# A row-wise nan-max on one core: the first load issued as three strided parts instead of one

## The chip, the cores and the metric

The kernel runs on one core of a Trainium2 chip. The metric is the device time of one execution in microseconds. The kernel before takes 1251.33 us (median of three runs, 1251.32 to 1251.34).

Four engines of the core matter here: ACT (ScalarE), POOL (GpSimd) and DVE (VectorE) compute, and SP (SyncE) issues all transfers. The transfers are carried out by 16 DMA engines.

## The reference

The input x is 32 x 2048 x 2048 in float32, drawn from a normal distribution, with one value in ten replaced by NaN. The output is the maximum over the last axis without the NaNs:

```python
def reference(x: np.ndarray, axis: int) -> np.ndarray:
    return np.nanmax(x, axis=axis).astype(np.float32)
```

These are 65536 rows of 2048 values (8 KB each), 537 MB in all, and 0.26 MB of results.

## The kernel before

**Tiles.** The rows are laid out over 128 partitions in five groups (`GROUPS`), so that a partition holds a run of neighbouring rows. Tiles go over a group from left to right. The unit is a quarter row (`Q` = 512 values). `TILES` lists for each tile its loads, its key chunks, and its reductions, all in quarter rows. Tile 0 is small: one row per partition, `[4]`, which is 1 MB and one load. Most of the others have 28 quarter rows, seven rows per partition, 7 MB in one load. Towards the end the loads are cut ever smaller, down to a quarter row in the last tile.

**Work on a tile.** Three steps remove the NaNs in place. ACT makes a 16-bit key from the upper half of each value (`act` with Prelu, into `kts`). POOL, or ACT for some chunks, turns the keys back into the upper halves (`write`), in which a NaN has become a very low number. DVE reduces each row to its maximum (`maxima`, into `accs`). After a group's last tile, `find_part` marks rows that held nothing but NaN, and six stores write the results.

**Buffers.** Three buffers `xts` hold tiles in turn, and three buffers `kts` hold keys. A tile's load may start when the last reduction of the tile that had the buffer is through (`free`).

**Order.** Everything but the first load stands in one critical section in which the order on each engine and all semaphores are made by hand: `Order.add` issues an instruction with the waits that it needs. An instruction that waits for several semaphores gets a separate wait instruction for each but the last. Loads use 14 semaphores in turn, the lanes (`LANES`, `lanes`, `turn`): a load waits for the load that had its lane before it.

**The first load.** `HEADS` is 1: tile 0's load is issued by SP ahead of the section (line 269), with a dependence offset that keeps the framework from ordering it against the buffer's later uses. Then comes the barrier at which the section begins (line 276); the other engines and SP's next loads (line 466) start behind it. Within the section the loop over tiles takes the already issued instruction from `heads` and adds it to the order as a load on lane 0, so that tile 0's key pass (line 282) waits for that lane.

Of the kernel before, what the change touches and what calls it, by code (L numbers as in the profile page):

```python
# [9 lines left out]
D = 2048  # L10

Q = D // 4
# [55 lines left out]
WIDE = 7  # L68
# [5 lines left out]
LEAD = 128  # L74

HEADS = 1

LANES = 14

# [13 lines left out]
def joints(keys, backs, reds):  # L93


    parts = []
    pieces = []
    at = end = step = 0
    for n, wait in backs:
        end += n  # L100
        while at < end:
            at += keys[step]
            step += 1
        if wait is None or wait >= 0:
            parts.append((end - n, end, wait is not None, step + (wait or 0), len(pieces)))
        pieces.append(n)
    needs = []
    done = 0
    for n in map(abs, reds):
        over = [i for i, p in enumerate(parts) if p[0] < done + n and p[1] > done]  # L110
        done += n
        pools = [i for i in over if not parts[i][2]]
        acts = sorted((i for i in over if parts[i][2]), key=lambda i: parts[i][3])
        if pools and acts and parts[pools[-1]][3] > parts[acts[-1]][3]:
            acts = []
        needs.append(pools[-1:] + acts[-1:])
    pairs = {}
    for need in needs:
        if len(need) == 2 and all(sum(i in n for n in needs) == 1 for i in need):
            both = tuple(parts[i][4] for i in need)  # L120
            for i in both:
                pairs[i] = both
    return pairs
# [62 lines left out]
def kernel(  # L186
# [15 lines left out]
    nc = tc.nc  # L202
    P = nc.NUM_PARTITIONS
# [14 lines left out]
    for tiles in GROUPS:  # L218
        at = 0
# [8 lines left out]
    firsts = [  # L228
        nc.alloc_sbuf_tensor(f"xt{i}", [P, WIDE * D], i32).ap() for i in range(HEADS)
    ]  # L230
# [6 lines left out]
    xts = firsts + [  # L237
        sing.tile([P, WIDE * D], i32, name=f"xt{i}") for i in range(HEADS, BUFS)
    ]
# [10 lines left out]
    groups = []  # L250
# [12 lines left out]
    order = Order(nc)  # L263
    heads = []
    for number in range(HEADS):
        (c,) = TILES[number][0]
        gi, base = place[number]
        to = xts[number][:, 0 : c * Q]
        head = nc.sync.dma_start(  # L269
            out=dataclasses.replace(to, dep_tracking_offset=to.offset + P * WIDE * D),  # L270
            in_=groups[gi][0][:, base : base + c * Q],
        )
        tc.no_tile_sem_insts.add(head.ins.name)
        heads.append(head)

    with tc.tile_critical() as section:  # L276

# [52 lines left out]
        lanes = [[] for _ in range(LANES)]  # L330
        turn = 0
# [43 lines left out]
        def freed(*ks):  # L375

            uses = [(back, then, e) for k in ks for back, ((_, then), e) in kfree[k].items()]
            counts = [e[1] for _, _, e in uses if e[0] == "pool"]
            deps = []
            for back, then, e in uses:  # L380
                if back == "act" and order.count["act"] >= then:
                    e = ("act", then)
                if back != "pool" or e[0] == "pool" or all(v < then for v in counts):
                    deps.append(e)
            return deps
# [39 lines left out]
        def find_part(i):  # L425
            gi, lo, hi = spans[i]
            first = groups[gi][2]
            acc = accs[:, first + lo : first + hi]
            deps = [done_at[PARTS[i][2]]]
            if PARTS[i][3] == "dve":  # L430
                none = nones[:, 0 : hi - lo]
                ready[i] = find("dve", nc.vector, deps, acc, none, ALU.bitwise_or)
            else:
                none = late[:, 0 : hi - lo]
                ready[i] = find("pool", nc.gpsimd, deps, acc, none, ALU.add)

        for number, (loads, chunks, reds) in enumerate(TILES):
            keys = [k for ks, _ in chunks for k in ks]
            fresh = {}
            step = 0  # L440
            for ks, bs in chunks:
                assert sum(ks) * Q <= KEYS
                assert sum(ks) == sum(b[0] if isinstance(b, tuple) else b for b in bs)
                fresh[step] = sum(ks) * Q
                step += len(ks)
            backs = [b for _, bs in chunks for b in bs]
            backs = [b if isinstance(b, tuple) else (b, None) for b in backs]
            assert sum(loads) == sum(keys) == sum(b for b, _ in backs) == sum(map(abs, reds))
            pairs[number] = joints(keys, backs, reds)
            for i, part in enumerate(PARTS):  # L450
                if part[3] == number:
                    find_part(i)
            gi, base = place[number]
            xg = groups[gi][0]
            xt, before = xts[number % BUFS], free[number % BUFS]
            assert number < BUFS or state["tile"] > number - BUFS
            landed = []
            at = 0
            for c in loads:
                c *= Q  # L460
                e = order.add(
                    "sp",
                    nc.sync,
                    lambda: heads[number]
                    if number < HEADS
                    else nc.sync.dma_start(  # L466
                        out=xt[:, at : at + c], in_=xg[:, base + at : base + at + c]
                    ),
                    before + lanes[turn],
                    lane=f"load{turn}",  # L470
                    step=16,
                )
                lanes[turn] = [e]
                turn = (turn + 1) % LANES
                landed.append((at, at + c, e))
                at += c
            end = at
            at = lo = part = 0
            for step, c in enumerate(keys):
                c *= Q  # L480
                here = [l for a, b, l in landed if a < at + c and b > at]
                kold = []
                if used + fresh.get(step, 0) > KEYS:
                    key = (key + 1) % NKEYS
                    used = 0
                    assert all(h[3] != key for h in held)
                    assert all(q[2] != key for v in half.values() for q in v)
                    kold = freed(key, (key + 1) % NKEYS) if number in EARLY and at + c == end else freed(key)
                    kfree[key] = {}
                e_key = act(  # L490
                    kold + here,
                    out=kts[key][:, used : used + c],
                    in_=xt[:, at : at + c].bitcast(i16)[:, 1::2],
                    func=ACT.Prelu,
                    bias=EDGE,
                    scale=-1.0,
                    alpha=float(TOP - LOW) / (EDGE - NAN),
                )
                used += c
                at += c  # L500
                for h in held:
                    h[-1] -= 1
                for h in [h for h in held if h[-1] <= 0]:
                    held.remove(h)
                    write(*h[:-1], "act")
                while backs and lo + backs[0][0] * Q <= at:
                    n, wait = backs.pop(0)
                    n *= Q
                    kp = kts[key][:, used - (at - lo) : used - (at - lo) + n]
                    if wait is not None and wait > 0:  # L510
                        held.append([number, lo, lo + n, key, kp, e_key, part, wait])
                    else:
                        who = "pool" if wait is None else "act" if wait == 0 else "dve"
                        write(number, lo, lo + n, key, kp, e_key, part, who)
                    lo += n
                    part += 1
                if number == len(TILES) - 1 and at == end:
                    for h in held:
                        write(*h[:-1], "act")
                    held.clear()  # L520
                maxima(number)
            assert lo == end
# [5 lines left out]
        for (gi, lo, hi), e in zip(spans, ready):  # L528
            _, og, first, _ = groups[gi]
# [4 lines left out]
                    out=og[:, lo:hi], in_=accs[:, first + lo : first + hi].bitcast(i32),  # L534
# [3 lines left out]
                lane="store",  # L538
                step=16,
# [47 lines left out]
```

## Time and profile before

| | |
|---|---|
| median of three runs | 1251.33 us |
| the profiled execution's own time | 1251.31 us |
| its span, first to last instruction | 1249.7 us |
| DMA engines, share of the span | 99.5% |
| mean rate over the span | 430 GB/s |
| POOL busy | 93% |
| DVE busy | 89% |
| ACT busy | 78% |

The span runs from the first to the last instruction that the profiler saw; what lies between it and the execution's time (1.6 us) is around the kernel. Lines such as L269 are lines of the kernel. "SPq" is SP's queue of DMA issues: its durations are those of issuing, not of moving data. A row of the timeline gives start, duration, engine, line, operation, destination and source with their shapes, the number of merged instructions, and in brackets the idle time before it and what ended it. A row of the waits gives who waited for whom, the sum, the number of times and the longest wait. A row of the stages gives the stretch, its length, the busy time and count of DVE, ACT and POOL, the granted clock, the DMA engines' busy share and the rate. A packet counts with all its bytes and its whole time in the stage in which it starts, so in short stages a share can be above 1.

### The profile page before, as it was taken

What the parts mean: (1) busy time and instruction counts of PE and PEld (TensorE: products, weight loads), DVE (VectorE), ACT (ScalarE), POOL (GpSimd) and SP (SyncE); (2) the same over time, 40 slices, a digit from 0 to 9 for tenths busy, and PEclk for the clock granted to TensorE, in tenths of its full rate; (3) what the DMA queues carried; (4) which work ended last, traced back from release to release, by engine and by line L of the source; (5) the groups of instructions that cost most, each with busy time, mean ns of one, the idle gap of its engine ahead of it and who ended that gap; (6) DMA issues with size and microseconds to landing.
All of it is one profiled execution on the core that took longest, in us unless ns stands there. A gap on an engine that the chain in (4) does not pass through costs nothing.

```text
span 1249.7 us, 920 instructions
## 1 busy us (share of the span) xinstructions
DVE 1109.7 (89%) x184; ACT 980.1 (78%) x286; POOL 1158.9 (93%) x256
## 2 busy tenths in 40 slices
DVE  0888889888889888888988888988898999999999
ACT  3777777777777777777777777799877799999998
POOL 2999999999999999999999999967999987999998
DMA  9999999999999999999999999999999999999997
GB/s 415 441 428 424 441 441 437 415 441 441 439 426 428 441 439 433 422 439 441 439 426 428 441 439 435 426 433 441 439 428 426 441 437 431 425 436 428 429 428 313
DMA packets 16854, 537.19 MB, mean 430 GB/s; under 512 B 2640, under 2 KB 2640, under 8 KB 5200
## 3 DMA queue, kind: packets, MB, share of 16 engines
q1 hardware_dynamic: 16848, 537.14, 99.5%
q14 instruction: 6, 0.05, 0.0%
HBM read 536.87 MB, written 0.26 MB: 430 GB/s over the span
## 4 chain that ended last, share of the span: by engine, by line
POOL 34%; DVE 30%; DMA 26%; ACT 9%; issue 1%; SPq 0%
POOL xt L292 34%; DVE acc L299 30%; DMA xt<-in_x_dram 26%; ACT kt L282 7%; ACT xt L282 2%; POOL late L305 0%; POOL acc L319 0%; SPq L269 0%; SPq L466 0%; DVE none L305 0%; DVE acc L319 0%; SPq L582 0%; SPq L276 0%
## 5 line engine op out<-in xcount | busy, mean ns | idle before, releaser
L292 POOL TENSOR_SCALAR xt<-kt 128x3584 int16<-128x3584 uint16 (+10 forms) x241 | 1153.9, 4788 | 84.5 <-ACT kt L282 69.3
L299 DVE TENSOR_REDUCE acc<-xt 128x4 f32<-128x8192 f32 (+4 forms) x182 | 1109.4, 6148 | 137.5 <-POOL xt L292 130.6
L282 ACT ACTIVATE kt<-xt 128x3584 uint16<-128x3584 int16 (+10 forms) x252 | 913.9, 3663 | 262.3 <-DMA xt<-in_x_dram 225.0
L282 ACT ACTIVATE xt<-kt 128x512 int16<-128x512 uint16 (+7 forms) x32 | 68.6, 2145 | 0.7
L305 POOL TENSOR_SCALAR late<-acc 128x112 int32<-128x112 f32 (+1 forms) x5 | 2.8, 558 | 0.4
L319 POOL TENSOR_TENSOR acc<-acc,late 128x112 int32<-128x112 int32 (+1 forms) x5 | 2.0, 397 | 0.4
L282 ACT ACT_TABLE_LOAD x1 | 1.3, 1283 | 1.3 <-SPq L276 1.3
L325 POOL MEMSET scalars<- 128x1 f32 x1 | 0.1, 98 | 1.0 <-SPq L276 1.0
L568 POOL MEMSET const-float32-0.0<- 128x1 f32 x1 | 0.1, 98 | 0.2 <-issue 0.2
L282 ACT ACTIVATE scalars<-scalars 128x1 f32<-128x1 f32 x1 | 0.2, 203 | 0.0
L305 DVE TENSOR_SCALAR none<-acc 128x7 int32<-128x7 f32 x1 | 0.2, 169 | 0.0
L319 DVE TENSOR_TENSOR acc<-acc,none 128x7 int32<-128x7 int32 x1 | 0.2, 161 | 0.0
L568 POOL MEMSET const-bfloat16-1.0<- 128x1 bf16 x1 | 0.1, 101 | 0.0
L568 POOL MEMSET const-uint8-127<- 128x1 uint8 x1 | 0.1, 101 | 0.0
L568 POOL MEMSET const-float32-1.0<- 128x1 f32 x1 | 0.1, 98 | 0.0
## 6 DMA issues: line engine op xcount, KB each, us to landing
xt<-in_x_dram SPq DMA_DIRECT2D x62, 7168.0 KB, 22.6
xt<-in_x_dram SPq DMA_DIRECT2D x2, 4096.0 KB, 19.4
xt<-in_x_dram SPq DMA_DIRECT2D x2, 3584.0 KB, 25.6
xt<-in_x_dram SPq DMA_DIRECT2D x5, 1280.0 KB, 29.4
xt<-in_x_dram SPq DMA_DIRECT2D x4, 1536.0 KB, 24.2
xt<-in_x_dram SPq DMA_DIRECT2D x2, 3072.0 KB, 26.3
xt<-in_x_dram SPq DMA_DIRECT2D x1, 5632.0 KB, 19.5
xt<-in_x_dram SPq DMA_DIRECT2D x2, 2816.0 KB, 24.8
```

The source lines that it names most:

```text
L282: lambda: nc.scalar.activation(**kw),
L292: lambda: nc.gpsimd.tensor_scalar(**kw),
L299: return order.add("dve", nc.vector, lambda: do(**kw), deps)
L305: lambda: engine.tensor_scalar(out=none, in0=acc, scalar1=NONE, scalar2=float(0x00800000), op0=ALU.is_equal, op1=ALU.mult,),
L319: lambda: engine.tensor_tensor(out=bits, in0=bits, in1=none, op=op),
L325: e_top = order.add("pool", nc.gpsimd, lambda: nc.gpsimd.memset(top, EDGE), [])
L568: nc = _bacc.Bacc("TRN2", target_bir_lowering=False, num_devices=1)
```

## The change

Tile 0's load is issued as three transfers, ahead of the section as before: the partitions 0, 4, 8 and so on (32 of them), the partitions 2, 6, 10 and so on (32), and all odd ones (64). Each moves the same 8 KB row per partition as before. In the section the three take one lane each, 0 to 2, and all later loads move on by two lanes. Tile 0's key pass waits for all three.

```diff
+PHASES = ((0, 4), (2, 4), (1, 2))
...
         to = xts[number][:, 0 : c * Q]
-        head = nc.sync.dma_start(
-            out=dataclasses.replace(to, dep_tracking_offset=to.offset + P * WIDE * D),
-            in_=groups[gi][0][:, base : base + c * Q],
-        )
-        tc.no_tile_sem_insts.add(head.ins.name)
-        heads.append(head)
+        heads.append([])
+        for first, step in PHASES:
+            part = to[first::step]
+            head = nc.sync.dma_start(
+                out=dataclasses.replace(
+                    part, dep_tracking_offset=part.offset + P * WIDE * D
+                ),
+                in_=groups[gi][0][first::step, base : base + c * Q],
+            )
+            tc.no_tile_sem_insts.add(head.ins.name)
+            heads[number].append(head)
...
-                e = order.add(
-                    "sp",
-                    nc.sync,
-                    lambda: heads[number]
-                    if number < HEADS
-                    else nc.sync.dma_start(
+                issues = [
+                    lambda: nc.sync.dma_start(
                         out=xt[:, at : at + c], in_=xg[:, base + at : base + at + c]
-                    ),
-                    before + lanes[turn],
-                    lane=f"load{turn}",
-                    step=16,
-                )
-                lanes[turn] = [e]
-                turn = (turn + 1) % LANES
-                landed.append((at, at + c, e))
+                    )
+                ]
+                if number < HEADS:
+                    issues = [lambda head=head: head for head in heads[number]]
+                for issue in issues:
+                    e = order.add(
+                        "sp",
+                        nc.sync,
+                        issue,
+                        before + lanes[turn],
+                        lane=f"load{turn}",
+                        step=16,
+                    )
+                    lanes[turn] = [e]
+                    turn = (turn + 1) % LANES
+                    landed.append((at, at + c, e))
```

## The prediction

> **What bounds the kernel now.** I read the page's totals first, then stages, waits and the end of the chain, and the first microseconds last, because the change is there.
>
> ```profile
> span 1249.7 us, 920 instructions
> DVE 1109.7 (89%) x184; ACT 980.1 (78%) x286; POOL 1158.9 (93%) x256
> ...
> q1 hardware_dynamic: 16848, 537.14, 99.5%
> q14 instruction: 6, 0.05, 0.0%
> ```
>
> No engine is busy all the time; the 16 DMA engines are (99.5%). The stages show whether that holds throughout (columns: stage, its length, busy us and count of DVE, ACT and POOL, clock, DMA share, GB/s):
>
> ```profile
> 20.00:1060.00 1040.00, 920.42 (x124) 797.40 (x196) 983.11 (x189) 1.00 1.00 434
> 1060.00:1200.00 140.00, 139.80 (x37) 134.92 (x48) 130.22 (x37) 1.00 1.00 430
> ```
>
> Up to 1060 us the stream moves 434 GB/s without a hole while all three engines have idle time. From 1060 on DVE is busy for 139.80 of 140 us. The waits of the two stages agree; the first two rows are of the stretch 40 to 1054 us and of SP over the whole span, the third of 1055 to 1249 us:
>
> ```profile
> ACT kt L282 <- DMA xt<-in_x_dram: 202.4, 53, 4.8
> ```
> ```profile
> SPq L466 <- DVE acc L299: 1151.4, 70, 37.9
> ```
> ```profile
> DVE acc L299 <- POOL xt L292: 0.2, 1, 0.2
> ```
>
> In the bulk ACT, which makes the keys, waits for a landing 53 times, 202.4 us together. SP's 1151.4 us looks larger, but is harmless: a load is issued when DVE frees its buffer, and lands a median of 22.6 us later,
>
> ```profile
> xt<-in_x_dram SPq DMA_DIRECT2D x62, 7168.0 KB, 22.6
> ```
>
> while its own 7.34 MB take 16.9 us at 434 GB/s. So at each issue some 5.7 us of earlier work still lies in the queues. The chain of waits and the timeline show where the stream stops setting the time:
>
> ```profile
> 1054.74 12.34 ACT L282 ACTIVATE kt<-xt 128x4096 uint16<-128x4096 int16 x3 [0.28 <-DMA xt<-in_x_dram]
> 1058.44 14.45 POOL L292 TENSOR_SCALAR xt<-kt 128x4096 int16<-128x4096 uint16 x3 [3.95 <-ACT kt L282]
> ```
> ```profile
> 1068.08 169.86 DVE acc L299 x52
> 1237.95 8.93 DVE acc L299 x4
> ```
>
> A load lands, ACT starts at 1054.74, POOL follows, and DVE reduces from 1068.08 to 1246.88 without a break. The time is therefore: start of the stream, its length up to the slowest engine's share of the load landing at 1054.7, and then 192 us of compute (1246.88 minus 1054.74) with the last store behind it. Only the start lies within reach of the change, and what it gains or loses there passes to the end one for one, since every key pass waits for its landing.
>
> **The change part by part.** The first microseconds, from the timeline, and then by stage:
>
> ```profile
> 0.72 0.39 SPq L269 DMA_DIRECT2D xt<-in_x_dram  x1
> 1.34 1.28 ACT L282 ACT_TABLE_LOAD   x1 [1.34 <-SPq L276]
> ...
> 2.63 0.20 ACT L282 ACTIVATE scalars<-scalars 128x1 f32<-128x1 f32 x1
> 5.49 1.91 ACT L282 ACTIVATE kt<-xt 128x2048 uint16<-128x2048 int16 x1 [2.65 <-DMA xt<-in_x_dram]
> ...
> 22.48 7.12 ACT L282 ACTIVATE kt<-xt 128x3584 uint16<-128x3584 int16 x2 [15.09 <-DMA xt<-in_x_dram]
> ```
> ```profile
> 1.38 0.33 SPq L466 DMA_DIRECT2D xt<-in_x_dram  x1
> ```
> ```profile
> 1.60:1.70 0.10, 0.00 (x0) 0.10 (x1) 0.00 (x0) 1.00 0.00 0
> 1.70:2.20 0.50, 0.00 (x0) 0.50 (x1) 0.00 (x0) 1.00 1.44 262
> 2.20:2.40 0.20, 0.00 (x0) 0.20 (x1) 0.00 (x0) 1.00 0.00 0
> 2.40:2.90 0.50, 0.00 (x0) 0.42 (x2) 0.00 (x0) 1.00 0.89 360
> 2.90:4.60 1.70, 0.00 (x0) 0.00 (x0) 0.00 (x0) 1.00 0.97 410
> 4.60:5.20 0.60, 0.00 (x0) 0.00 (x0) 0.00 (x0) 1.00 3.73 1598
> 5.20:6.70 1.50, 0.00 (x0) 1.21 (x1) 0.00 (x0) 1.00 0.00 0
> ```
>
> A packet is booked in the stage in which it starts. From 1.70 to 2.20, 262 GB/s for 0.5 us are 131 KB: 16 packets of 8 KB (a partition's row), one for each DMA engine. None starts in the next 0.2 us; then all go on at full rate. So the engines start one after another over nearly 0.5 us. From 4.60 to 5.20 they pass to the next load, again spread over at most 0.6 us: the late starter stays late. The slowest engine's stream begins up to 0.5 us behind the first's, and a landing waits for the slowest.
>
> *Step 1, a smaller first part.* The 128 rows (eight for each of 16 engines) become 32, 32 and 64, with the bytes unchanged. If the stagger grows with the rows that are handed out, a quarter of the rows leave a quarter of it: 0.12 of 0.5 us, and the last engine starts 0.37 us earlier. If it is something else (cold memory), the gain is 0. If the first packet also comes earlier, it is at most the 0.39 us of the issue on top: a bound of 0.37 + 0.39 = 0.76. What counts is the engine that is slowest at 1054.7, which need not have started last; a middle one would gain about half of 0.37, which is 0.19. I take 0.25, between the two.
>
> *Step 2, two more issues on SP ahead of the barrier.* What a back-to-back issue costs, one store and then two in the timeline of the end:
>
> ```profile
> 1242.31 0.34 SPq L533 DMA_DIRECT2D out_dram<-acc  x1
> ```
> ```profile
> 1242.31 0.82 SPq L533 DMA_DIRECT2D out_dram<-acc  x2
> ```
>
> The second adds 0.48 us. The two parts thus come 0.48 and 0.96 us after the first, at 1.20 and 1.68, and the barrier and the 7 MB load move from 1.38 to about 2.34. Are the engines fed? From issue (0.72) to first packet (1.70) are 1.0 us, so part two can start at 2.2 and part three at 2.7. Part one keeps an engine from 1.70 to about 2.8, by two packets (the first until 2.40 or later, the second 0.31 us, 8 KB at 1/16 of 434 GB/s); part two holds until 3.4. Part three is there 0.7 us early. The large load can start at 3.3, and the engines need it at 4.60. Expected cost 0; were this cover gone (the engines run dry at both seams), the two issues would cost 0.96 us.
>
> *Step 3, what waits behind the barrier.* ACT's table load goes from 1.34 to 2.30 and its warm-up ends at 3.8 rather than 2.83, still before the landing at 5.49. POOL's scalar is earlier still. Cost 0; without cover 0.96 us on the first tile alone, and then ACT's 15.09 us of waiting for tile 1 would absorb it.
>
> *Step 4, three semaphores instead of one.* The first key pass waits for three landings. Queued behind it on ACT is the pass at 22.48, which waits 15.09 us; POOL and DVE have only this tile. Cost 0 up to 15 us.
>
> *Step 5, lanes.* The three parts take lanes 0 to 2, and every later load moves two lanes on. A load still waits for the fourteenth before it, as now, and the head has landed 200 us before its lanes return (14 loads of 16.9 us). Cost 0, also in the tail, where the distance and the sizes are the same.
>
> *Step 6, instruction fetch.* The six packets on q14 hold 0.05 MB, some 8 KB each, and one costs its DMA engine 0.31 us by the rate above. A few more instructions on SP and ACT may move one to or from the slowest engine: between -0.3 and +0.3, taken as 0.
>
> The sum against the profiled execution's own 1251.31 us (span 1249.7, 1.6 around it; median of the runs 1251.33): 1251.31 - 0.25 = 1251.06, rounded to 1251.1.
>
> **The rivals.**
>
> A: the stagger is not of the hand-out; time 1251.3. For it: nothing in the profile tells cold memory from handing out. Against: the starts come evenly, not in a bunch, and the spread persists.
>
> B, the slower side: each part pays a start of its own. By the rows that is 1.0 us from issue to packet; where parts two and three can't start before their predecessor is through, 2 × 1.0 us go into the stream: 1253.3. It decides as soon as a queued transfer doesn't follow on directly. Against it: the 7 MB load, queued behind the head, starts in 4.60 to 5.20, before the head's landing was seen at 5.49, with no hole between. [...]
>
> C: the parts spread badly over the destination. If two engines write through one path at a time, the head's 1.05 MB go at half of 434 GB/s and take 2.4 us longer: 1253.7. [...]
>
> D: the parts arrive late or at a seam the engines run dry, 0.1 to 0.96 us: about 1251.8, the middle. Against: the margins of 0.7 and 1.3 us in step 2.
>
> E: more gain than the forecast, where the first packet comes earlier too: 1250.55 to 1250.85.
>
> **How the numbers follow.** Forecast (gain of 0.1 to 0.46): 50%. A: 22%. D: 12%. E: 7%. B: 4%. C: 5%. The range of 8 in 10 goes from 1250.5 (E's bound) to 1252.0; it leaves out B, C and tails of D and step 6. About 2.5 us (0.2%) separates a difference from none in this kernel. The forecast, A, D, E and B lie inside that. C with a share of D would pass it: 3% slower. Faster by 2.5 us would need more than the whole 1 us before the first packet and the stagger together: 2%. Within: 95%.
>
> **What would show it.** Right: in 1.70 to 2.20 the 16 first packets are bunched in 0.1 to 0.2 us; no hole before 4.60; the burst into tile 1 ends before 5.1; ACT's first pass starts at about 5.2 and the one at 22.48 some 0.25 us earlier; the same shift at 1054.74 and at the last reduction. A shows in an unchanged spread and an unmoved 22.48; D or B in stages under 400 GB/s at 2.2 to 3.4; C in packets twice as long up to 5 us. I am wrong if the shift at 22.48 isn't the shift at the end, which would mean that the slowest engine at 1054.7 is made later on, or if the stream's 434 GB/s changes.

## The result, and the profile after

The changed kernel takes 1253.51 us (median of 22 runs, 1252.72 to 1254.34), the kernel before in the same runs 1251.34 (1251.27 to 1251.92). The ratio is 1.0017, with a 95% interval from 1.0011 to 1.0023: 2.2 us slower, where a gain of 0.25 and a range of 1250.5 to 1252.0 were forecast. The profiled execution is one of the longer ones, 1254.13 us with a span of 1252.4, so the profiles differ by 2.7 us in span and the medians by 2.2.

The page's totals after, and the two stages of the bulk (columns as before):

```profile
span 1252.4 us, 923 instructions
DVE 1109.7 (89%) x184; ACT 980.2 (78%) x286; POOL 1159.1 (93%) x256
...
q1 hardware_dynamic: 16880, 537.14, 99.4%
q14 instruction: 6, 0.05, 0.0%
```
```profile
20.00:1060.00 1040.00, 917.76 (x124) 794.79 (x195) 981.73 (x188) 1.00 1.00 434
1060.00:1200.00 140.00, 139.76 (x36) 135.35 (x47) 129.31 (x36) 1.00 1.00 430
```

Work and rates are the same: 434 and 430 GB/s in the two stages, the busy times over the whole span within 0.2 us, six packets of instruction fetch as before. So the loss should lie ahead of 20 us. The timeline of the start and of the load that lands near 1055, and the chain's last piece:

```profile
0.72 1.82 SPq L274 DMA_DIRECT2D xt<-in_x_dram  x3
2.77 1.28 ACT L289 ACT_TABLE_LOAD   x1 [2.77 <-SPq L283]
...
2.81 12.53 SPq L469 DMA_DIRECT2D xt<-in_x_dram  x3
...
8.21 1.91 ACT L289 ACTIVATE kt<-xt 128x2048 uint16<-128x2048 int16 x1 [3.94 <-DMA xt<-in_x_dram]
...
25.17 7.12 ACT L289 ACTIVATE kt<-xt 128x3584 uint16<-128x3584 int16 x2 [15.05 <-DMA xt<-in_x_dram]
```
```profile
1057.43 12.34 ACT L289 ACTIVATE kt<-xt 128x4096 uint16<-128x4096 int16 x3 [0.29 <-DMA xt<-in_x_dram]
```
```profile
1070.76 178.83 DVE acc L306 x56
```

ACT's pass on tile 1 starts at 25.17 instead of 22.48, its pass near 1055 at 1057.43 instead of 1054.74, and the last reduction ends at 1249.59 (1070.76 plus 178.83) instead of 1246.88. That is 2.69, 2.69 and 2.71 us: what the start loses arrives at the end, one for one. The whole difference is made before tile 1 has landed. Where, the stages show:

```profile
1.60:2.00 0.40, 0.00 (x0) 0.00 (x0) 0.00 (x0) 1.00 0.00 0
2.00:2.60 0.60, 0.00 (x0) 0.00 (x0) 0.00 (x0) 1.00 0.71 218
2.60:2.90 0.30, 0.00 (x0) 0.13 (x1) 0.09 (x1) 1.00 1.00 355
2.90:4.60 1.70, 0.00 (x0) 1.36 (x2) 0.01 (x1) 1.00 0.88 284
4.60:5.20 0.60, 0.00 (x0) 0.00 (x0) 0.00 (x0) 1.00 1.38 546
5.20:6.70 1.50, 0.00 (x0) 0.00 (x0) 0.00 (x0) 1.00 1.29 481
```

Three things differ. The first packets come after 2.0 us instead of 1.7, and no closer together: 218 GB/s for 0.6 us are again 16 packets, but some of these are already the second of their engine. Counted from the packets of the trace, 16 are under way at once, one for each engine, from 2.84 us on, and in the kernel before from 2.19. From 2.90 to 4.60 the rate is 284 GB/s instead of 410, at a busy share of 0.88 instead of 0.97. Two things lie behind that. Some engines have no packet, and the packets take longer: those that start in this stage last 0.40 us in the mean in the trace, 0.31 in the kernel before (8 KB each). Finer stages show where engines run dry, first of the kernel before, then of the change:

```profile
2.90:3.50 0.60, 0.00 (x0) 0.00 (x0) 0.00 (x0) 1.00 1.00 423
3.50:4.10 0.60, 0.00 (x0) 0.00 (x0) 0.00 (x0) 1.00 1.00 423
4.10:4.60 0.50, 0.00 (x0) 0.00 (x0) 0.00 (x0) 1.00 0.89 377
```
```profile
2.90:3.50 0.60, 0.00 (x0) 0.60 (x1) 0.01 (x1) 1.00 0.93 369
3.50:4.10 0.60, 0.00 (x0) 0.59 (x2) 0.00 (x0) 1.00 0.72 191
4.10:4.60 0.50, 0.00 (x0) 0.17 (x1) 0.00 (x0) 1.00 1.00 295
```

By 3.66 us the first 64 of tile 0's 128 packets have started, as many as parts one and two have, so the dip to 0.72 lies at the seam to part three. Between 3.6 and 4.6 us 11.4 of the 16 engines have a packet in the mean of the time, in the kernel before all 16. And the burst into tile 1, which was over by 5.20, is smeared to beyond 6.70: the engines have come apart, and a landing waits for the last of them.

The trace's packets also divide the loss. On each engine a load ends with a packet of 4 bytes (the two added transfers add 32 packets to q1, 16 each). Those of tile 1 end between 21.56 and 22.16 us in the kernel before, 21.80 in the mean, and between 22.42 and 24.81 us in the change, 23.28 in the mean. The mean engine is thus 1.48 us later. By 20 us it has been without a packet for 0.90 us longer than before, of which the later first packet makes 0.33, and its packets have taken 0.57 us longer. The last engine is 2.65 us later: a further 1.2 us are lost because it has fallen behind the mean. ACT's pass on tile 1 starts 0.36 us behind it, in the kernel before 0.32.

### The profile page after: what moved, and what is told of

It is laid out like the page before. It is cut to its first block, busy times and chain, and to the rows that moved or that the text cites. A ratio compares the mean times of both kernels' runs of the same rounds, so it can differ in the third digit from the quotient of the medians.

```text
span 1252.4 us, 923 instructions
## 1 busy us (share of the span) xinstructions
DVE 1109.7 (89%) x184; ACT 980.2 (78%) x286; POOL 1159.1 (93%) x256
## 4 chain that ended last, share of the span: by engine, by line
POOL 34%; DVE 30%; DMA 26%; ACT 9%; issue 1%; SPq 0%
POOL xt L299 34%; DVE acc L306 30%; DMA xt<-in_x_dram 26%; ACT kt L289 7%; ACT xt L289 2%; SPq L274 0%; POOL late L312 0%; POOL acc L326 0%; SPq L469 0%; DVE none L312 0%; DVE acc L326 0%; SPq L593 0%; SPq L283 0%
```

## The experiments

Times are medians of ten runs beside runs of the kernel before on the same chip (medians 1251.30 to 1251.49, all runs within 1251.18 to 1251.72). e1 to e4 ran on one chip, e5 to e8 on a second, e9 to e16 on a third, e17 and e18 on a fourth; a comparison across these groups changes the chip too. "Tile 1" is the start of ACT's first pass on tile 1 in the profile, which is of a single run: of the fastest or nearly so in e2, e6 and e11, of the slowest in e16. With so few runs the interval of a ratio is about 0.001 to either side, 1.2 us; differences of half a microsecond rest on the ranges of runs, and profile and median need not agree to better than that.

| Run | Median (range) us | Over before | Tile 1, us |
|---|---|---|---|
| e1 three parts of 128 rows | 1252.92 (1252.38 to 1253.87) | +1.43 | 24.44 |
| e2 even and odd | 1252.40 (1252.24 to 1253.66) | +0.91 | 23.55 |
| e3 other group, three parts | 1253.78 (1252.96 to 1254.05) | +2.29 | 24.30 |
| e4 other group, one part | 1251.65 (1251.43 to 1251.80) | +0.16 | 22.67 |
| e5 odd rows first | 1252.74 (1252.17 to 1253.55) | +1.40 | 24.43 |
| e6 long part first | 1252.20 (1251.36 to 1252.74) | +0.86 | 22.50 |
| e7 short part first | 1251.67 (1251.52 to 1252.12) | +0.33 | 22.97 |
| e8 two halves of the row | 1252.52 (1251.74 to 1252.82) | +1.18 | 23.97 |
| e9 tile 1 issued later | 1251.48 (1251.19 to 1252.24) | +0.18 | 22.65 |
| e10 three parts, tile 1 early | 1253.76 (1252.58 to 1254.71) | +2.46 | 25.43 |
| e11 halves, tile 1 early | 1251.93 (1251.44 to 1252.37) | +0.63 | 22.34 |
| e12 one part, tile 1 early | 1251.32 (1251.22 to 1251.47) | +0.02 | 22.44 |
| e13 tiles 10, 20, 30, 40 in parts | 1251.40 (1251.31 to 1251.53) | +0.03 | 22.41 |
| e14 tile 1 in parts | 1251.57 (1251.37 to 1252.16) | +0.20 | 22.47 |
| e15 parts from SP and ACT | 1251.95 (1251.85 to 1252.57) | +0.58 | 23.35 |
| e16 halves from SP and ACT | 1251.45 (1251.30 to 1251.84) | +0.08 | 23.11 |
| e17 halves, tile 1 issued later | 1251.84 (1251.68 to 1252.16) | +0.50 | 22.73 |
| e18 halves, tile 1 from ACT | 1252.13 (1251.93 to 1252.63) | +0.79 | 25.13 |

### Is it the rows, the added transfers, or the place in memory?

e1, all 128 partitions in every part, with a piece of the row each:

```diff
-PHASES = ((0, 4), (2, 4), (1, 2))
+PHASES = ((0, 512), (512, 1024), (1024, 2048))
...
-            part = to[first::step]
+            part = to[:, first:step]
...
-                in_=groups[gi][0][first::step, base : base + c * Q],
+                in_=groups[gi][0][:, base + first : base + step],
```

> The first load still goes out as three transfers ahead of the section, but each takes all 128 partitions: the first 512 values of the row, the next 512, the last 1024 (the same bytes per part as the strided split). Three theories of the 2.7 us by which the strided split is late at tile 1's landing (25.15 against 22.46 us). Rows (a part with 32 or 64 of the 128 rows is handed to the DMA engines so that they get in each other's way): the packets keep their full rate, tile 1 lands within 0.4 us of 22.46, time 1251.0 to 1251.7. Issues (every added transfer costs a start, or the engines run dry between parts): as slow as the strided split, tile 1 at 24.4 or later, time 1253 to 1254. Source (the strided parts read memory at a distance that memory serves badly): as for rows, 1251.0 to 1251.7.

e2: `PHASES = ((0, 2), (1, 2))`.

> Two parts of 64 partitions each, the even and the odd ones. Rows: as slow as the three parts or nearly, since every part is short of rows: packets of 8 KB over 0.5 us, tile 1 lands at 24.2 to 25.2 us, time 1252.8 to 1254. Issues: one added transfer instead of two, half the loss, tile 1 at 23.8, time 1252.4 to 1252.7. Source: the rows of a part are 1 MB apart instead of 2 MB in the first two, a smaller loss, 1252 to 1253.

e3 and e4 move tile 0 to the first group, e3 with the change's parts, e4 with one:

```diff
-    tuple(range(1, 17)),
+    tuple(range(0, 17)),
...
-    (0,) + tuple(range(65, 74)),
+    tuple(range(65, 74)),
...
-    (0, 1, 16, 18),
+    (0, 0, 16, 18),
...
-    (4, 0, 72, None),
+    (4, 65, 72, None),
```

> The strided three parts as in the change, but tile 0 is moved from the last group (64 rows to a partition, so that neighbouring partitions' rows lie 512 KB apart in memory) to the first group (113 rows, 904 KB apart). Source: the loss goes; tile 1 lands within 0.5 us of the one-part kernel with the same groups, packets of 8 KB take some 0.31 us. Rows and issues: the loss stays at 2 to 2.7 us at tile 1's landing, packets over 0.5 us as before.

> The kernel before with tile 0 in the first group (113 rows to a partition), as the measure for the strided split with these groups. All theories: the first load in one part runs at full rate as before, tile 1 lands at 22.3 to 22.7 us, time 1251.0 to 1252.0 (what the tail's new place in memory does is not known).

With 904 KB between neighbouring partitions' rows instead of 512 the parts cost 2.13 us (e3 over e4), as in the change: it is not this distance in memory. Parts with all 128 partitions still lose 1.43 of the change's 2.2 (e1): by this pair the rows are the smaller share. (The shorter packets of e1 explain little of it. In its trace 2 KB take 84 ns and 4 KB 159, against 309 for 8 KB, an estimate of 0.14 us for an engine's share of tile 0.) The stages of e1:

```profile
2.60:2.90 0.30, 0.00 (x0) 0.30 (x1) 0.00 (x0) 1.00 0.94 321
2.90:4.60 1.70, 0.00 (x0) 0.87 (x2) 0.00 (x0) 1.00 0.93 300
4.60:5.20 0.60, 0.00 (x0) 0.00 (x0) 0.00 (x0) 1.00 1.96 669
5.20:6.70 1.50, 0.00 (x0) 0.00 (x0) 0.00 (x0) 1.00 1.34 453
```

This is much of the change's picture, 300 GB/s and a smeared burst, without a strided row in it. Its dip is shallower: between 3.6 and 4.6 us 14.1 of the 16 engines have a packet. One added transfer costs less than two (e2).

### Does every added transfer cost, or a part that comes late?

e5: `PHASES = ((1, 2), (0, 4), (2, 4))`. e6, e7 and e8 as e1, with `((0, 1792), (1792, 2048))`, `((0, 256), (256, 2048))` and `((0, 1024), (1024, 2048))`.

> The same three strided parts, the 64 odd partitions first and the two parts of 32 behind them. Late (the engines run out of work at a seam because the next part's issue, 0.61 us apart, comes just as a part of 32 rows, two packets of 0.31 us for an engine, is through): the first part now lasts 1.24 us for an engine, so the first seam is covered and only the second is open; tile 1 lands at 23.2 to 24.0 us, time 1252.1 to 1252.9. Each (every added transfer costs the engines about 1 us, wherever it stands): as the change, tile 1 at 24.3 to 25.2, time 1253.0 to 1254. Neither is excluded by the landing alone if it lies between.

> Two parts of 128 partitions: the first 1792 of the row's 2048 values, then the last 256. Late: the first part lasts 2.1 us for an engine, the second is issued 0.43 us behind it; no seam is open, tile 1 lands at 22.4 to 22.8 us, time 1251.3 to 1251.7. Each: one added transfer costs 1 us as with the even and odd parts, tile 1 at 23.3 to 23.7, time 1252.2 to 1252.6.

> Two parts of 128 partitions: the first 256 values of the row, then the other 1792. Late: the first part lasts 0.3 us for an engine, the second comes 0.43 us behind it, so the seam is open for 0.1 to 0.6 us; tile 1 at 22.6 to 23.1 us, time 1251.5 to 1252.1. Each: tile 1 at 23.3 to 23.7, time 1252.2 to 1252.6.

> Two parts of 128 partitions, the two halves of the row. Late: the first part lasts 1.2 us for an engine, the second is issued 0.43 us behind it; no seam is open, tile 1 at 22.4 to 22.8 us, time 1251.3 to 1251.7. Each: tile 1 at 23.3 to 23.7, time 1252.2 to 1252.6, as with the even and odd parts; the difference from those is what rows cost beside the added transfer.

Neither theory holds throughout. Late holds for the short first part: e7 lies inside its range, and in the trace of e7 the engines are without a packet for 0.23 us longer than in the kernel before. For the odd rows first it holds by the time alone, since tile 1 comes later in e5 than its 24.0 us. It fails for the long first part and the halves, which were to cover their seams and lost 0.86 and 1.18 in the median (the profile of e6, with tile 1 at 22.50, is of a run without the loss, 1251.36). A fixed price for each transfer fails too, with 0.33, 0.86, 0.91 and 1.18 for one. And with two parts strided rows lost no more than full ones (0.91 in e2, 1.18 in e8). The stages of e8 show where the two halves lose:

```profile
2.60:2.90 0.30, 0.00 (x0) 0.30 (x1) 0.00 (x0) 1.00 1.00 396
2.90:4.60 1.70, 0.00 (x0) 0.39 (x2) 0.00 (x0) 1.00 1.03 412
4.60:5.20 0.60, 0.00 (x0) 0.00 (x0) 0.00 (x0) 1.00 3.37 1038
5.20:6.70 1.50, 0.00 (x0) 0.73 (x1) 0.00 (x0) 1.00 0.61 235
```

The second half follows the first without a hole, at 396 and 412 GB/s. The loss is behind it, where tile 1's packets start: 1038 GB/s in the burst instead of 1598, and stragglers up to 6.70. Between 4.6 and 5.8 us only 12.3 of the 16 engines have a packet, although tile 1's load was issued at 1.84, and its first packet on each engine (56 KB) takes 2.76 us in the mean instead of 2.12.

### Is tile 1's load late?

e9 is the kernel before with one wait more, which holds tile 1's load until ACT's warm-up is through:

```diff
-        act([e_top], out=warm, in_=top, func=ACT.Prelu, alpha=0.5)
+        e_warm = act([e_top], out=warm, in_=top, func=ACT.Prelu, alpha=0.5)
...
-                    before + lanes[turn],
+                    before + lanes[turn] + ([e_warm] if number == 1 else []),
```

> The first load in one part as before; only the next load, tile 1's 7 MB, waits for ACT's warm-up and so is issued at about 2.9 us instead of 1.38, as late as in the change (2.81). No transfer is added. Next load late (it needs some 3 us of lead over the moment at which the engines are through with the first load, not the 1.0 us that the first packet takes): the engines stall at the hand-over, tile 1 lands at 23.2 us or later, time 1252.1 to 1253.2. Each (what costs is the added transfer): tile 1 at 22.4 to 22.8 us, time 1251.2 to 1251.6.

e10, e11 and e12 issue tile 1's load ahead of the section too (`HEADS = 2`, tile 1 in one part), behind the change's parts, behind the two halves, and behind one part.

> The three strided parts as in the change, but tile 1's load is issued with them ahead of the section (at about 2.6 us, some 0.25 earlier than in the change). Next load late: a little better than the change, by 0 to 0.3 us: 1253.2 to 1253.5. Each: as the change, 1253.2 to 1253.8. This is the measure beside the next one more than a test by itself.

> The first load as two halves of the row, 128 partitions each, and tile 1's load ahead of the section right behind them, at about 1.6 us instead of 1.84: a lead of about 2.95 us over the hand-over at 4.5 instead of 2.7. Next load late: the stall at the hand-over goes from 0.7 us towards 0.2, tile 1 lands at 22.5 to 23.2 us, time 1251.4 to 1252.0. Each: as without, tile 1 at 23.3 to 24.0 us, time 1252.2 to 1252.6.

> The kernel before with tile 1's load issued ahead of the section, right behind the first load, at about 1.15 us instead of 1.38. Next load late: before has no stall at the hand-over, so nothing is gained: 1251.1 to 1251.6. Each: the same.

In e9 the load is issued at 2.86 us, later than in the change:

```profile
2.86 9.63 SPq L466 DMA_DIRECT2D xt<-in_x_dram  x3
...
22.65 3.19 ACT L282 ACTIVATE kt<-xt 128x3584 uint16<-128x3584 int16 x1 [15.39 <-DMA xt<-in_x_dram]
```

It costs 0.18 us. So the later issue alone isn't the cause, and the earlier issue alone gains nothing (e12). The earlier issue doesn't help the three parts either (e10). Behind the halves it took off half the loss (e11), though the ranges of e8 and e11 overlap and the chips differ.

### Does splitting cost elsewhere, and from two queues?

e13 issues four tiles in mid-stream in the change's three parts, the first load in one; e14 the same for tile 1 alone (`number == 1`):

```diff
-                    lambda: nc.sync.dma_start(
-                        out=xt[:, at : at + c], in_=xg[:, base + at : base + at + c]
-                    )
+                    lambda first=first, step=step: nc.sync.dma_start(
+                        out=xt[first::step, at : at + c],
+                        in_=xg[first::step, base + at : base + at + c],
+                    )
+                    for first, step in (PHASES if number in (10, 20, 30, 40) else ((0, 1),))
```

> The first load in one part as before; the 7 MB loads of the tiles 10, 20, 30 and 40 go out as the three strided parts instead (32, 32 and 64 partitions), eight added transfers, each with some 5 us or more of other work queued ahead of it. Short lead (an added transfer costs only where the queues hold little work ahead of it): 1251.3 to 1251.8. Each (about 0.7 to 1 us for every added transfer, anywhere): 1256 to 1260. Rows (strided parts go at half the rate): 8.5 to 17 us for each of the four tiles, 1285 or more.

> The first load in one part; tile 1's 7 MB load, issued behind the barrier at 1.4, 2.0 and 2.6 us, in the three strided parts. Its seams lie where the engines have worked for 4 and 8 us on the part before. Short lead: 1251.3 to 1251.7, tile 1 lands at 22.4 to 22.8 us. Each, or anything that is issued in the first 3 us: two added transfers, 1252.6 to 1253.8, tile 1 at 23.8 us or later.

e15 (the change's parts) and e16 (the halves of e8) issue the first part from SP and the others from ACT:

```diff
-            head = nc.sync.dma_start(
+            head = (nc.scalar if first else nc.sync).dma_start(
```

> The change's three strided parts, the first issued by SP and the other two by ACT at the same time, so that the barrier and tile 1's load come 0.6 us later instead of 1.2, and part two comes with part one. Short lead: the loss shrinks to about that of one added transfer, 1252.0 to 1252.8. Each: as the change, 1253.0 to 1254.

> The first load in the two halves of the row, 128 partitions each, one issued by SP and the other by ACT at the same time; tile 1's load is issued at 1.4 us as before. Short lead: neither part nor tile 1 comes late, 1251.2 to 1251.7, tile 1 at 22.3 to 22.8 us. Each: as two parts from one queue, 1252.0 to 1252.6.

Eight added transfers in mid-stream cost nothing. The issues of e13, with the twelve parts among them, and the bulk's rate, 433 GB/s against 434:

```profile
xt<-in_x_dram SPq DMA_DIRECT2D x58, 7168.0 KB, 22.6
xt<-in_x_dram SPq DMA_DIRECT2D x6, 3584.0 KB, 21.4
xt<-in_x_dram SPq DMA_DIRECT2D x10, 1792.0 KB, 13.2
```
```profile
20.00:1060.00 1040.00, 920.36 (x124) 797.30 (x196) 983.02 (x189) 1.00 1.00 433
```

Parts of 32 and 64 rows thus run at full rate where some 5 us of work is queued ahead of them. Issued in the first three microseconds, but for tile 1, whose parts are needed only from 4.6 us on, they cost 0.20 (e14). And the halves that lost 1.18 from one queue (e8, another chip) lose 0.08 from two (e16), the three parts 0.58 (e15).

### Is SP's queue slower than the issues?

e17 is e8 with e9's wait, e18 is e11 with tile 1's load from ACT's queue (`(nc.scalar if number else nc.sync)`).

> The two halves of the row from SP's queue as in the run with two halves (1252.5 us), and tile 1's load issued at about 3.3 us instead of 1.84, since it waits for ACT's warm-up. Queue slower than the issues (it takes some 1.6 us for each transfer in the cold start, so that tile 1's would reach the engines at about 4.9 us whether issued at 1.84 or 3.3): no further loss, 1252.2 to 1252.8. Issued late: 1.5 us later, so 1 to 1.5 us more: 1253.4 to 1254.

> The two halves from SP's queue, tile 1's load from ACT's queue at the same time as the first half. Queue slower than the issues: tile 1's load no longer stands behind the halves, no stall at the hand-over, 1251.2 to 1251.8. Issued late: the same, as it is issued at 0.72 us. An added transfer that costs by itself: 1252.2 to 1252.8.

Both went against the theory that they were made for. Held back to 3.33 us, tile 1's load does better than at 1.84 (0.50 lost instead of 1.18, with ranges that overlap and on another chip). The stages of e17:

```profile
2.90:4.60 1.70, 0.00 (x0) 0.39 (x2) 0.00 (x0) 1.00 0.98 398
4.60:5.20 0.60, 0.00 (x0) 0.00 (x0) 0.00 (x0) 1.00 4.12 1550
5.20:6.70 1.50, 0.00 (x0) 1.13 (x1) 0.00 (x0) 1.00 0.09 38
```

The burst into tile 1 is back (1550 GB/s, against 1038 in e8), and of tile 1's first packets only one starts later (38 GB/s from 5.20 to 6.70 are 57 KB). But the packets take longer: a share of 4.12 for 1550 GB/s, against 3.73 for 1598 in the kernel before. And taken from behind the halves to a queue of its own (e18), tile 1's load leaves a loss of 0.79; tile 0's pass then waits for the halves until 23.31 us (5.97 in e8), as it would if the packets of tile 1 ran between theirs, and tile 1's pass stands behind it (25.13 us, in the row below the second of three merged passes):

```profile
23.31 8.92 ACT L289 ACTIVATE kt<-xt 128x2048 uint16<-128x2048 int16 x3 [20.01 <-DMA xt<-in_x_dram]
```

No variant beats the kernel before; e12 and e13 equal it.

## Why the prediction was wrong, step by step

**What bounds the kernel: right.** The stream does up to the load near 1055, and a shift of the start reaches the end unchanged (2.69, 2.69, 2.71 us).

**Step 1 (gain 0.25): wrong.** The stagger of the first packets didn't shrink with the rows: 16 are under way 0.77 us after the first packet, against 0.46 in the kernel before. That speaks against the number of rows handed out as its cause. Rival A's doubt about the stagger was right, its time of 1251.3 was not.

**Step 2 (cost 0): the step that failed.** It took the second issue's 0.48 us and the 1.0 us from issue to first packet, both from rows of transfers with 128 partitions, and concluded that the engines are fed without a hole and at full rate, part three being there 0.7 us early. Instead the engines ran dry at the seam to part three (191 GB/s at a share of 0.72 from 3.50 to 4.10), the packets took longer, and the engines came apart. The margin had one small error: parts of 32 or 64 rows took longer to issue. Here are the three issues of e1, against 1.82 for three issues in the change:

```profile
0.72 1.32 SPq L274 DMA_DIRECT2D xt<-in_x_dram  x3
```

The first packet came at 2.06 us in the change and at 1.74 in the kernel before (in e1, with 128 rows first, ahead of 2.00, with 46 GB/s from 1.60 to 2.00). A part of these 0.3 us goes into the difference between the change and e1 (0.7 us). It doesn't use up the margin. Issued at some 1.9 us, and with the 1.34 us from issue to packet that part one needed, part three would have been there at about 3.3, an estimate, while packets of parts one and two started up to 3.66; why it came later isn't shown. The large error is the price of 0 for a seam: 284 GB/s in the change, 300 in e1 with all 128 partitions in every part, and the three shares of the loss above (0.90 us without a packet, 0.57 of longer packets, 1.2 of the last engine behind the mean). Full rate right behind a seam had been read from tile 1's load, which follows a single transfer; that row didn't show what several do.

**Rival B** (each part pays a start of its own, 2.0 us, 1253.3) came within 0.2 us of the measured time by luck, on a wrong count: by e13 a part behind other work pays nothing, and by e7, e6, e2 and e8 one part pays 0.3 to 1.2. The runs show 2.2 us for two added transfers at the start and 0.03 for eight in mid-stream.

**Rival C** (a bad spread over the destination, 2.4 us) had the size too, but e1 loses 1.43 us without strided rows and e13 has strided rows without a loss (0.03). That two engines share one path was an assumption; no run shows it.

**Rival D** was what step 2 had to fear, bounded by 0.96 us, the time of two issues. It came true in part: the engines were without a packet for 0.90 us longer, which is inside the bound. The longer packets and the engines' coming apart lie outside it, so its time was too low. Its sign, a stage under 400 GB/s at 2.2 to 3.4 us, decides nothing, since the kernel before has 360 GB/s from 2.40 to 2.90; the dry stretch came later.

**Steps 3 and 4: right.** The barrier moved to 2.8 us and the first pass to 8.21, and nothing behind felt it. In e15, where the odd rows on ACT's queue landed 15.7 us after their issue, that pass started at 17.02 us,

```profile
17.02 1.91 ACT L289 ACTIVATE kt<-xt 128x2048 uint16<-128x2048 int16 x1 [13.15 <-DMA xt<-in_x_dram]
```

and the run lost only 0.58. **Step 5:** no other cost appeared. **Step 6:** six fetches, as before.

**What stays open.** The runs show where the loss is made (ahead of tile 1's landing, most of it in the first 8 us), that it comes with added transfers in a queue that has just started and not with every added transfer (e13), and that it is neither the distance in memory (e3) nor the late issue of the next load alone (e9). In the change the trace shows what it consists of. Three causes are not shown: why part three's packets, and tile 1's in e8, reached some engines late; why packets then take longer; and why the same kernel loses anything from nothing to 1.4 us (e6, 1251.36 to 1252.74). That holding back the large load helps (e17) and that a second queue helps the halves (e16) but not the large load (e18) would fit transfers that disturb each other in the engines. But this is argued, not shown, and rests on runs of different chips.

## What to carry to other kernels

Price a split by where it stands: with 5 us of work queued ahead, splitting loads into strided parts cost nothing here (0.03 us, e13), while at the empty queues of the start the same split cost 2.2 us. The cost of zero, read from one transfer following another, didn't carry over to several small ones at the start (2.2 us); bound such a cost by the whole start, not by the issue's time. Cut the stages fine when you look for a hole: a share of 0.88 over 1.70 us hid a dip to 0.72 over 0.60 us. In this kernel, whose stream sets the time up to 1055 us, what the start lost arrived at the end (2.69 us at tile 1, 2.71 at the last reduction).

## What the hardware showed unexpectedly

An issue of 32 or 64 rows took longer than one of 128: the first issue of the change and of the kernel before,

```profile
0.72 0.55 SPq L274 DMA_DIRECT2D xt<-in_x_dram  x1
```

0.55 against 0.39 us; the 64 odd rows took 0.59 in the change, as the third issue, and 0.57 in e5, as the first. Whether the number or the stride of the partitions makes this, no run separates. And the first microseconds of a stream are a place of their own: the same strided parts ran at 284 GB/s there and without a loss in mid-stream (e13), and tile 1's first packet on each engine took 2.36 us in the mean in the change, 2.69 in e1 and 2.76 in e8, against 2.12 in the kernel before.
